# HGRN sample tokens in whole-array products: value copies by transfers, scores from the key copies, a score tile per head

## The chip, the core and the metric

The kernel runs on one core of a Trainium2 chip. The engines that matter here are TensorE (PE in the profile; its weight loads are the row PEld), VectorE (DVE), ScalarE (ACT), GpSimd (POOL) and SyncE (SP), which issues most transfers. The metric is the device time of one execution in microseconds; times are medians of several runs. TensorE is an array of 128 x 128 cells. A matrix product can use a part of it: the profile writes 128\*128 for the whole array, 32\*128 for a tile of 32 rows, 128\*32 for a tile of 32 columns.

## What is computed

One inference step of a hybrid layer: 1024 prompt tokens and 8 sample sequences of 4 tokens each (32 sample tokens), width 1024. After an RMS norm one projection feeds two groups, HGRN2 (4 heads, keys and values of 128) and a gated convolution; both are merged by the output projection. The change concerns the HGRN2 recurrence of the sample tokens. For each sequence and head, with g the running sum of log f within the 4 tokens:

```
g = cumsum(logf)
decay = exp(where(causal, g[t] - g[s], -inf))
scores[t,s] = sum_d q[t,d] k[s,d] decay[t,s,d]
o[t]  = sum_s scores[t,s] v[s]  +  (q[t] * exp(g[t])) @ s0
s_new = exp(g_last) * s0 + sum_s (k[s] * exp(g_last - g[s])) v[s]^T
```

The eight sequences are independent of one another; each begins from a state s0 that is an input.

## The kernel before

Everything lies with features on the 128 partitions and tokens along the free axis: 1024 prompt columns and 32 sample columns beside them, cut into three blocks of 352 for a projection. The input projection runs as 24 blocks of 128 output features (`order`: gates and values of the convolution gb and ga, forget f and query q per head, then za and zb), each a sum of 72 products in `fp32r` (weights and inputs are split into a high and a low part, three products each). Weights come by one transfer a block (`load_w`), are cast to the high part by ScalarE and reduced to the low part by VectorE. Four PSUM banks (`mm`) hold the projections, two (`aux`) the small products, one each `ops` and `ptps`.

Beside the projections run two lists of work written as Python generators: `hq`, the HGRN heads (`hgrn`), and `bg`, the convolution and its norm. After each third of a projection `pump` takes three steps (`HU`) of the first list, and steps of the second as long as a modelled clock of VectorE is not too far ahead of TensorE's. A step ends at a `yield`. What is emitted in this order is then placed by a planner, which simulates the engines with its own costs: earlier emitted work goes first where it is ready, and each engine keeps the planned order. Buffers of a tag are handed out in the order of emission.

A head first does the prompt in two halves of 512 tokens, stores the prompt's state, and then does the sample part:

- it loads the eight states s0 (tile `raw`, a single buffer, which later also holds blocks of the output weights);
- `ki` holds g less its last value per sequence; after an exponential and a product with k it is written four times side by side (`k4`, 128 x 4 x 32), and turned by TensorE, so that the four copies of the 32 tokens lie on the 128 partitions (`kT`);
- the head's values lie in 32 rows of `vs` (head hd in rows 32 hd to 32 hd + 31). A product with `bones` (ones where two indices are the same token) spreads them to four copies in PSUM. ScalarE casts keys and values to `fp32r`, VectorE puts the rounding rest in some of the copies (`kT`, `vr`), so that one pass of products gives the full precision;
- the scores: `base` makes a second pair of decayed operands, from g less its value at the second token (two exponentials, a difference, two products); a product in a tile of 32 columns gives 32 x 32 scores in the head's rows, and a masked copy puts the causal ones within a sequence into `ptss`, one 128 x 32 tile for all heads;
- the outputs: a product of the head's 32 rows of `vs` with the same rows of `ptss` in a tile of 32 rows, plus what the states give (sixteen small products with `qz`, copied to `isb`, and a product with `bones`);
- the state update: the values are masked per sequence (`vm`), two products with `kT` give the sums, VectorE adds them to the decayed s0, and the result is stored.

The tiles `v4`, `k4`, `kT`, `vr` and `isb` share the tag `kts`. The output projection waits for all heads and the convolution's norm.

Of the kernel before, what the change touches and what calls it, by code (L numbers as in the profile page):

```python
# [9 lines left out]
F32 = mybir.dt.float32  # L10
BF16 = mybir.dt.bfloat16
F32R = mybir.dt.float32r
U8 = mybir.dt.uint8
I32 = mybir.dt.int32
AF = mybir.ActivationFunctionType
ALU = mybir.AluOpType
AX = mybir.AxisListType

P = 128
# [3 lines left out]
NS = 4  # L23
ST = NB * NS
# [3 lines left out]
H = 4  # L28
# [28 lines left out]
NMASK = 2 + len(LEVELS)  # L57
# [39 lines left out]
def emit(nc, tc, h, fast, flag_out=None):  # L97
    HW = 5
    with ExitStack() as ctx:
# [5 lines left out]
        def sb(shape, tag, bufs=1, dt=F32):  # L105
            return pool.tile(shape, dt, tag=tag, name=tag, bufs=bufs)
# [4 lines left out]
        def bank(tag, bufs):  # L111
            return psp.tile([P, 512], F32, tag=tag, name=tag, bufs=bufs)
# [4 lines left out]
        def aux():  # L117
            return bank("aux", 2)

        S = nc.scalar  # L120
        V, T = Clock(nc.vector, _dve_ns), Clock(nc.tensor, _pe_ns)
# [18 lines left out]
        vs = sb([P, P], "vs")  # L140
# [186 lines left out]
        smask = sb([P, nmask, ST], "smask", dt=U8)  # L327
# [16 lines left out]
        pts = [sb([P, 2, P], "pt%d" % i) for i in range(2)]  # L344
# [5 lines left out]
            nc.gpsimd.memset(t, 0.0)  # L350
        bones = sb([P, P], "bones")
        nc.sync.dma_start(bones, h["bones"])
        ptss = sb([P, ST], "pts")
        nc.gpsimd.memset(ptss, 0.0)


# [105 lines left out]
        def hgrn(hd, q, k, g):  # L462
            vcols = slice(hd * P, (hd + 1) * P)
            rows = slice(hd * ST, (hd + 1) * ST)
            ptps = late["ptps"]
            st = None
            if fast:

                gc = g[:, 0:SEQ].rearrange("p (c t) -> p c t", t=P)
                r0, r1 = rng[:, hd, 0:8], rng[:, hd, 8:16]  # L470
# [7 lines left out]
            for hf in range(2):  # L478
                c0 = hf * 512
                gv = g[:, c0 : c0 + 512]  # L480
                qv = q[:, c0 : c0 + 512]
                kv = k[:, c0 : c0 + 512]

                def hw():
                    return sb([P, 512], "hw", HW)

                def rel(blk, idx, src=gv, n=512, mk=hw):
                    d = mk()
                    v = src.rearrange("p (c t) -> p c t", t=blk)
                    V.tensor_tensor(  # L490
                        d.rearrange("p (c t) -> p c t", t=blk),
                        v,
                        v[:, :, idx : idx + 1].to_broadcast([P, n // blk, blk]),
                        ALU.subtract,
                    )
                    return d

                def level(hs, src=gv, n=512, mk=hw, qq=qv, kk=kv):
                    blk = 2 * hs
                    d = rel(blk, hs - 1, src, n, mk)  # L500
                    d3 = d.rearrange("p (c t) -> p c t", t=blk)
                    q3 = qq.rearrange("p (c t) -> p c t", t=blk)
                    k3 = kk.rearrange("p (c t) -> p c t", t=blk)
                    l, r = slice(0, hs), slice(hs, blk)
                    S.activation(d3[:, :, l], d3[:, :, l], AF.Exp, scale=-1.0)
                    S.activation(d3[:, :, r], d3[:, :, r], AF.Exp)
                    V.tensor_tensor(d3[:, :, l], d3[:, :, l], k3[:, :, l], ALU.mult)
                    V.tensor_tensor(d3[:, :, r], d3[:, :, r], q3[:, :, r], ALU.mult)
                    return d

                def base(blk, idx, src=gv, n=512, mk=hw, qq=qv, kk=kv):
                    d = rel(blk, idx, src, n, mk)
                    kb = mk()
                    S.activation(kb, d, AF.Exp, scale=-1.0)
                    S.activation(d, d, AF.Exp)
                    V.tensor_tensor(kb, kb, kk, ALU.mult)
                    V.tensor_tensor(d, d, qq, ALU.mult)
                    return d, kb
# [4 lines left out]
                if fast:  # L523


                    qb, kb = base(P, P // 2 - 1)
                    yield
                    kps = aux()
                    for c in range(4):
                        T.transpose(kps[:, c * P : (c + 1) * P], kb[:, c * P : (c + 1) * P], ident)  # L530
                    kT = sb([P, 512], "ho", 2)
                    S.copy(kT, kps)
                    for c in range(4):
# [5 lines left out]
                            start=True, stop=True,  # L539
# [3 lines left out]
                            start=True, stop=True, tile_position=(0, 64),  # L543
# [19 lines left out]
                    for c in range(4):  # L563
                        T.matmul(
                            dps[:, c * P : (c + 1) * P],
                            lhsT=kT[:, c * P : (c + 1) * P],
                            rhs=vt[:, hf * 4 + c, vcols],
                            start=True,
                            stop=True,
# [14 lines left out]
                else:  # L584
# [3 lines left out]
                    ki = hw()  # L588
# [9 lines left out]
                    kps = aux()  # L598
                    for c in range(4):
                        T.transpose(kps[:, c * P : (c + 1) * P], ki[:, c * P : (c + 1) * P], ident)  # L600
                    kT = sb([P, 512], "ho", 2)
# [3 lines left out]
                    for c in range(4):  # L605
                        T.matmul(
                            dps[:, c * P : (c + 1) * P],
                            lhsT=kT[:, c * P : (c + 1) * P],
                            rhs=vt[:, hf * 4 + c, vcols],
                            start=True,  # L610
                            stop=True,
# [14 lines left out]
                    for i, hs in enumerate(LEVELS + (0,)):  # L626
                        if hs:
                            a = b = level(hs)
                        else:
                            a, b = kv, qv  # L630
                        for c in range(4):
                            T.matmul(
                                ptps[:, c * P : (c + 1) * P],
                                lhsT=a[:, c * P : (c + 1) * P],
                                rhs=b[:, c * P : (c + 1) * P],
                                start=True,
                                stop=True,
# [15 lines left out]
                for c in range(4):  # L653
                    oc = ops[:, c * P : (c + 1) * P]
                    if sts[c] is not None:
                        T.matmul(
                            oc, lhsT=sts[c], rhs=qi[:, c * P : (c + 1) * P], start=True, stop=False
# [3 lines left out]
                        lhsT=vt[:, hf * 4 + c, vcols],  # L661
                        rhs=pts[c // 2][:, c % 2, :],
                        start=(sts[c] is None),
                        stop=True,
# [11 lines left out]
            gv, qv, kv = (t[:, SEQ:TOK] for t in (g, q, k))  # L676

            def sm():
                return sb([P, ST], "sm", 8)

            s0 = sb([P, NB, P], "raw", 1)
            nc.sync.dma_start(s0, h["sh"][hd])
            eg = sb([P, NB], "egs", 2)
            S.activation(eg, gv.rearrange("p (c t) -> p c t", t=NS)[:, :, NS - 1], AF.Exp)
            ki = rel(NS, NS - 1, gv, ST, sm)
            S.activation(ki, ki, AF.Exp, scale=-1.0)
            k4 = sb([P, 4, ST], "kts", 3)
            V.tensor_tensor(
                k4,
                ki.unsqueeze(1).to_broadcast([P, 4, ST]),  # L690
# [2 lines left out]
            )  # L693
            kps = aux()
            T.transpose(kps[:, 0:P], k4.rearrange("p a t -> p (a t)"), ident)
            T.matmul(
                kps[:, P : 2 * P],
                lhsT=bones[rows, :],
                rhs=vs[rows, :],
                start=True,  # L700
                stop=True,
                tile_position=(hd * ST, 0),
            )


            kT = sb([P, P], "kts", 3, F32R)
            vr = sb([P, P], "kts", 3, F32R)
            S.copy(kT, kps[:, 0:P])
            S.copy(vr, kps[:, P : 2 * P])
            for dst, src, r0, r1 in ((kT, 0, 2, 4), (vr, P, 1, 2), (vr, P, 3, 4)):  # L710
                rr = slice(r0 * ST, r1 * ST)
                V.tensor_tensor(
                    dst[rr], kps[rr, src : src + P], dst[rr].bitcast(F32), ALU.subtract
                )
            qi = sm()
            S.activation(qi, gv, AF.Exp)
            qz = qzs[0]
# [4 lines left out]
                ALU.mult,  # L722
            )
            yield
            sps = aux()
            if fast:
                qb, kb = base(NS, 1, gv, ST, sm, qv, kv)
                pairs = [(kb, qb)]
            else:
                pairs = []  # L730
                for hs in LEVELS[-2:]:
                    a = level(hs, gv, ST, sm, qv, kv)
                    pairs.append((a, a))
                pairs.append((kv, qv))
            for i, (a, b) in enumerate(pairs):
                sp = sps[rows, i * ST : (i + 1) * ST]
                T.matmul(sp, lhsT=a, rhs=b, start=True, stop=True, tile_position=(0, hd * ST))
                mi = 0 if fast else NMASK - 3 + i
                V.copy_predicated(ptss[rows, :], smask[rows, mi, :], sp)
            ops = bank("ops", 1)  # L740
            T.matmul(
                ops[:, 0:ST],
                lhsT=vs[rows, :],
                rhs=ptss[rows, :],
                start=True,
                stop=False,
                tile_position=(hd * ST, 0),
            )
            ips = aux()
            for b in range(NB):  # L750
                j = b % 4
                T.matmul(
                    ips[j * ST : (j + 1) * ST, 0:P],
                    lhsT=qz[:, b * ST : (b + 1) * ST],
                    rhs=s0[:, b, :],
                    start=(b < 4),
                    stop=(b >= 4),
                    tile_position=(0, j * ST),
                )
            isb = sb([P, P], "kts", 3)  # L760
            S.copy(isb, ips[:, 0:P])
            T.matmul(ops[:, 0:ST], lhsT=isb, rhs=bones[:, 0:ST], start=False, stop=True)
            yield
# [486 lines left out]
def program(nc, tc, h, fallback=True):  # L1250
    with tc.tile_pool(name="flag", bufs=1) as fp:
        flag = fp.tile([1, 1], I32, name="flag")
        emit(nc, tc, h, True, flag)
        if fallback:
            slow = nc.values_load(flag[0:1, 0:1], min_val=0, max_val=1)
            with tc.If(slow > 0):
                emit(nc, tc, h, False)
# [98 lines left out]
```

## Time and profile before

| What | us |
|---|---|
| median of 3 runs | 500.35 (499.99 to 501.29) |
| the profiled execution | 500.03 |
| its span | 498.2 |
| the sample products of the four heads begin at | 184.2, 242.9, 309.2, 361.8 |
| first load of output weights issued (L1085) | 356.2 |

The mean granted clock of TensorE was 0.993. A row of the timeline gives the start, the length, the engine, the line (for most operations the line of a helper, L72), the operation, the tile written and the tiles read, the form and the number of instructions merged into the row; in brackets stands the idle time of the engine before it and what ended it. "issue" means that the engine waited for nothing that the profile shows. A product in full f32 appears as two instructions, one in `fp32r` as one. A group row gives smallest, median and largest length in ns, and the first and last start.

### The profile page before, as it was taken

The page shows a single profiled execution, that of the slowest core. Times are in us where ns is not written, and L with a number is a line of the kernel's source. Part 1 is how long each engine was busy: PE and PEld are TensorE (multiplying, and loading weights), DVE is VectorE, ACT ScalarE, POOL GpSimd, SP SyncE. Part 2 cuts the span into 40 slices and gives each one's busy share as a digit, 9 for nine tenths or more (in the row PEclk, how much of TensorE's full clock was granted, in tenths as well). Part 3 has the DMA queues.
Part 4 walks back from the last instruction along what each step waited for, and adds up shares of the span by engine and source line. Part 5 has one row for each costly group of instructions (what it writes and reads, how often), then busy time and mean ns, then how long its engine had stood idle before and what let it go on. Part 6 is the DMA issues. An engine that isn't in the chain of part 4 may idle for free.

```text
span 498.2 us, 7600 instructions
## 1 busy us (share of the span) xinstructions
PE 484.2 (97%) x3020; PEld 442.7 (89%) x3020; DVE 358.6 (72%) x682; ACT 250.6 (50%) x439; POOL 3.0 (1%) x20
## 2 busy tenths in 40 slices
PE   6999999999999999999999999999999999999992
PEld 5788899999999998999999999999999977877781
DVE  4864213999999989998999988993677747543441
ACT  5764332413646554635536554545766985422321
POOL 1000000000000000000000000000000000000000
PEclk9999999999999999999999999999999999999997
DMA  7910501231111213211123101131115396432111
GB/s 272 314 43 13 170 25 30 42 62 36 42 44 43 52 49 61 88 43 43 48 55 128 27 27 49 42 128 44 47 43 180 89 415 202 153 114 86 42 53 49
DMA packets 23003, 43.52 MB, mean 87 GB/s; under 512 B 10640, under 2 KB 11920, under 8 KB 22960
## 3 DMA queue, kind: packets, MB, share of 16 engines
q1 hardware_dynamic: 21808, 40.86, 26.3%
q10 hardware_dynamic: 1152, 2.10, 1.1%
q8 instruction: 25, 0.41, 0.3%
q14 instruction: 18, 0.15, 0.1%
HBM read 35.72 MB, written 7.24 MB: 86 GB/s over the span
## 4 chain that ended last, share of the span: by engine, by line
PE 90%; ACT 4%; DMA 3%; DVE 2%; issue 1%; SPq 0%; DVEq 0%
PE mm L72 70%; PE ops L72 8%; PE ptps L72 6%; PE aux L72 5%; DMA u<-gin 1%; ACT big L954 1%; DMA raw<-wo 1%; DMA o_hs<-raw 1%; DVE raw L72 1%; ACT L455 1%; DVE qkg L72 0%; ACT big L1100 0%; DVE big L72 0%; ACT qkg L455 0%; DVE u L72 0%
## 5 line engine op out<-in xcount | busy, mean ns | idle before, releaser
L72 PE MATMUL mm<-big,wh 128*128 128x352 f32 (+1 forms) x1280 | 323.7, 332 | 0.0
L72 PEld LDWEIGHTS mm<-big,wh 128*128 128x128 f32 x1280 | 224.1, 188 | 8.1 <-issue 1.6
L72 PE MATMUL mm<-big,wl 128*128 128x352 f32 (+1 forms) x640 | 211.4, 331 | 0.0
L72 PEld LDWEIGHTS mm<-big,wl 128*128 128x128 f32 x640 | 120.5, 188 | 3.4 <-issue 0.4
L72 DVE TENSOR_TENSOR wl<-wraw,wh 128x1024 fp32r<-128x1024 f32 x24 | 29.3, 1222 | 25.9 <-ACT wh L390 25.8
L72 DVE SCALAR_TENSOR_TENSOR big<-u,wsum,big 128x511 f32<-128x511 f32 (+14 forms) x60 | 44.5, 741 | 0.6
L72 DVE SCALAR_TENSOR_TENSOR big<-u,cols,big 128x511 f32<-128x511 f32 (+14 forms) x60 | 44.0, 735 | 0.0
L72 DVE SCALAR_TENSOR_TENSOR cq<-u,cols,cq 128x511 f32<-128x511 f32 (+13 forms) x56 | 41.2, 735 | 0.0
L72 DVE TENSOR_TENSOR qkg<-mm,big 128x512 f32<-128x512 f32 x16 | 10.9, 690 | 35.7 <-PE mm L72 35.7
L390 ACT CAST wh<-wraw 128x1024 fp32r<-128x1024 f32 x24 | 25.1, 1047 | 17.2 <-issue 7.8
L72 PE MATMUL mm<-vt,wh 128*128 128x512 f32 x64 | 25.6, 402 | 0.4 <-ACT wh L1167 0.4
L395 ACT ACT_TABLE_LOAD x20 | 25.7, 1283 | 0.3
L455 ACT ACTIVATE qkg<-mm 128x352 f32<-128x352 f32 x48 | 19.4, 465 | 11.4 <-PE mm L72 11.3
L72 PE MATMUL mm<-vt,wl 128*128 128x512 f32 x64 | 24.8, 390 | 0.0
L1204 ACT ACTIVATE big<-qkg 128x512 f32<-128x512 f32 x16 | 10.0, 628 | 29.1 <-DVE qkg L72 29.1
L455 ACT ACT_TABLE_LOAD x16 | 20.5, 1283 | 1.3 <-PE mm L72 1.0
L72 PE MATMUL ops<-big 128*128 128x512 f32 x64 | 20.8, 403 | 0.2 <-ACT big L197 0.2
L72 PE MATMUL ptps<-big 128*128 128x512 f32 x64 | 19.9, 394 | 0.0
L1167 ACT CAST wh<-big 128x512 fp32r<-128x512 f32 x16 | 9.2, 617 | 19.1 <-PE mm L72 18.6
L72 PEld LDWEIGHTS mm<-vt,wh 128*128 128x128 f32 x64 | 12.0, 188 | 5.2 <-ACT wh L1167 1.7
L72 PE MATMUL mm<-hw,wh 128*128 128x512 f32 x40 | 15.7, 392 | 0.0
L799 ACT ACTIVATE big<-aux,eps 128x512 f32<-128x512 f32 (+1 forms) x12 | 6.7, 556 | 17.9 <-PE aux L72 17.5
(239 smaller groups left out, 634.7 us busy)
## 6 DMA issues: line engine op xcount, KB each, us to landing
wraw<-win SPq DMA_DIRECT2D x24, 512.0 KB, 3.6
wraw<-wo SPq DMA_DIRECT2D x12, 512.0 KB, 3.7
big<-xp SPq DMA_DIRECT2D x2, 2048.0 KB, 10.1
big<-xp SPq DMA_DIRECT2D x4, 512.0 KB, 10.7
raw<-sh SPq DMA_DIRECT2D x4, 512.0 KB, 3.5
o_hs<-raw SPq DMA_DIRECT2D x4, 512.0 KB, 3.0
raw<-wo SPq DMA_DIRECT2D x4, 512.0 KB, 5.2
o_yp<-qkg ACTq DMA_DIRECT2D x8, 256.0 KB, 2.9
```

What stands on the lines that cost most here:

```text
L72: return f(*a, **k)
L390: S.copy(hi, wr)
L395: after(S.preload_act_table_set("natural_log_exp_and_others"), prev)
L455: return [S.activation(dst[:, nb * MB : (nb + 1) * MB], ps, func, bias=bias)]
L799: S.activation(r, ms[:, 0:n], AF.Ln, bias=eps)
L954: return S.activation(cv[:, c, cs], cv[:, c, cs], AF.Silu, bias=cols[:, C_LNB + c : C_LNB + c + 1], scale=cols[:, C_LNG + c : C_LNG + c + 1],)
L1167: S.copy(hv, m[:, :, ts])
L1204: S.activation(xr[:, hs], y[:, hs], AF.Square, accum_out=sqs[:, half : half + 1])
```

## The change

The values are no longer spread by a product: four transfers within SBUF copy the head's 32 rows of `vs` to a tile `v4`, ahead of a new `yield`. The scores take the four key copies `k4` as the stationary side, so that the product uses all 128 columns and gives the same scores in four groups of rows; only the head's own rows are copied out. The moving side is a new `qe`, the query times the exponential of `ki`. The score tile gets a place of 32 columns for each head and is zero outside the head's rows, so that the output product can run over all 128 rows of `vs`. The tag `kts` gets a fourth buffer. The fallback path (`fast` false) is kept to the same layout; it isn't executed with these inputs.

```diff
-        ptss = sb([P, ST], "pts")
+
+        ptss = sb([P, H, ST], "pts")
         nc.gpsimd.memset(ptss, 0.0)
...
             s0 = sb([P, NB, P], "raw", 1)
             nc.sync.dma_start(s0, h["sh"][hd])
+
+            v4 = sb([P, P], "kts", 4)
+            for j in range(4):
+                nc.sync.dma_start(v4[j * ST : (j + 1) * ST, :], vs[rows, :])
+            yield
             eg = sb([P, NB], "egs", 2)
             S.activation(eg, gv.rearrange("p (c t) -> p c t", t=NS)[:, :, NS - 1], AF.Exp)
             ki = rel(NS, NS - 1, gv, ST, sm)
+            if fast:
+                qe = sm()
+                S.activation(qe, ki, AF.Exp)
+                V.tensor_tensor(qe, qe, qv, ALU.mult)
             S.activation(ki, ki, AF.Exp, scale=-1.0)
...
             kps = aux()
             T.transpose(kps[:, 0:P], k4.rearrange("p a t -> p (a t)"), ident)
-            T.matmul(
-                kps[:, P : 2 * P],
-                lhsT=bones[rows, :],
-                rhs=vs[rows, :],
-                start=True,
-                stop=True,
-                tile_position=(hd * ST, 0),
-            )
...
-            S.copy(vr, kps[:, P : 2 * P])
...
+            if fast:
+
+                sps = kps[:, P : P + ST]
+                T.matmul(
+                    sps, lhsT=k4.rearrange("p a t -> p (a t)"), rhs=qe, start=True, stop=True
+                )
+                V.copy_predicated(ptss[rows, hd, :], smask[rows, 0, :], sps[rows, :])
...
+            S.copy(vr, v4)
...
-            sps = aux()
-            if fast:
-                qb, kb = base(NS, 1, gv, ST, sm, qv, kv)
-                pairs = [(kb, qb)]
...
             ops = bank("ops", 1)
             T.matmul(
                 ops[:, 0:ST],
-                lhsT=vs[rows, :],
-                rhs=ptss[rows, :],
+                lhsT=vs,
+                rhs=ptss[:, hd, :],
                 start=True,
                 stop=False,
-                tile_position=(hd * ST, 0),
             )
```

More of the change, by code (lines that the diff above doesn't have):

```diff
@@ L685, in hgrn @@
             ki = rel(NS, NS - 1, gv, ST, sm)
+            if fast:
+                qe = sm()
+                S.activation(qe, ki, AF.Exp)
+                V.tensor_tensor(qe, qe, qv, ALU.mult)
             S.activation(ki, ki, AF.Exp, scale=-1.0)
-            k4 = sb([P, 4, ST], "kts", 3)
+            k4 = sb([P, 4, ST], "kts", 4)
             V.tensor_tensor(
@@ L695, in hgrn @@
             T.transpose(kps[:, 0:P], k4.rearrange("p a t -> p (a t)"), ident)
-            T.matmul(
-                kps[:, P : 2 * P],
-                lhsT=bones[rows, :],
-                rhs=vs[rows, :],
-                start=True,
-                stop=True,
-                tile_position=(hd * ST, 0),
-            )
-            kT = sb([P, P], "kts", 3, F32R)
-            vr = sb([P, P], "kts", 3, F32R)
+            if fast:
[4 more added lines that the diff above has]
+                V.copy_predicated(ptss[rows, hd, :], smask[rows, 0, :], sps[rows, :])
+            vr = sb([P, P], "kts", 4, F32R)
+            S.copy(vr, v4)
+            kT = sb([P, P], "kts", 4, F32R)
             S.copy(kT, kps[:, 0:P])
-            S.copy(vr, kps[:, P : 2 * P])
-            for dst, src, r0, r1 in ((kT, 0, 2, 4), (vr, P, 1, 2), (vr, P, 3, 4)):
+            for dst, src, r0, r1 in ((kT, kps, 2, 4), (vr, v4, 1, 2), (vr, v4, 3, 4)):
                 rr = slice(r0 * ST, r1 * ST)
-                V.tensor_tensor(
-                    dst[rr], kps[rr, src : src + P], dst[rr].bitcast(F32), ALU.subtract
-                )
+                V.tensor_tensor(dst[rr], src[rr, 0:P], dst[rr].bitcast(F32), ALU.subtract)
             qi = sm()
@@ L724, in hgrn @@
             yield
-            sps = aux()
-            if fast:
-                qb, kb = base(NS, 1, gv, ST, sm, qv, kv)
-                pairs = [(kb, qb)]
-            else:
+            if not fast:
+                sps = aux()
                 pairs = []
@@ L734, in hgrn @@
                 pairs.append((kv, qv))
[L735 to L739, printed above, removed]
+                for i, (a, b) in enumerate(pairs):
+                    sp = sps[rows, i * ST : (i + 1) * ST]
+                    T.matmul(sp, lhsT=a, rhs=b, start=True, stop=True, tile_position=(0, hd * ST))
+                    V.copy_predicated(ptss[rows, hd, :], smask[rows, NMASK - 3 + i, :], sp)
             ops = bank("ops", 1)
@@ L759, in hgrn @@
                 )
-            isb = sb([P, P], "kts", 3)
+            isb = sb([P, P], "kts", 4)
             S.copy(isb, ips[:, 0:P])
```

## The prediction

> **What bounds the kernel now.** I read the page's busy line first, then the shares of the chain that ended last, then the table of stages, and last the timeline of TensorE around one head's sample part.
>
> ```profile
> PE 484.2 (97%) x3020; PEld 442.7 (89%) x3020; DVE 358.6 (72%) x682; ACT 250.6 (50%) x439; POOL 3.0 (1%) x20
> PE 90%; ACT 4%; DMA 3%; DVE 2%; issue 1%; SPq 0%; DVEq 0%
> 180.00:200.00 20.00, 20.00 (x144) 18.15 (x143) 18.75 (x41) 9.20 (x17) 0.12 (x1) 1.00 0.31 68
> ```
>
> TensorE is busy for 97% of the span and makes 90% of the last chain. The third line is the stage in which head 0's sample tokens are worked on (columns: window; its length; busy us and instructions of PE, PEld, DVE, ACT, POOL; granted clock; DMA share; GB/s): PE has no idle time at the full clock. VectorE, at 18.75 of 20 us, is close behind. So what the change is worth there is what it takes out of TensorE's row of products, as long as nothing else takes the lead.
>
> "Busy" hides something. A projection's wide products (352 columns) start every 0.16 us, a 512-column product takes 0.23 us to the next start, yet around small tiled products the row stretches. I price each small product by that stretch: from the last wide start ahead of it to the second wide start behind it, less what the same wide products take undisturbed.
>
> ```profile
> 184.24 0.27 PE L72 MATMUL aux<-ident,kts 128*128 128x128 f32 x1
> 184.44 0.48 PE L72 MATMUL aux<-vs,bones 32*128 32x128 f32 x2
> 184.85 0.43 PE L72 MATMUL mm<-big,wh 128*128 128x352 f32 x1
> 185.12 0.32 PE L72 MATMUL mm<-big,wl 128*128 128x352 f32 x1
> ...
> 189.38 0.32 PE L72 MATMUL mm<-big,wh 128*128 128x352 f32 x1
> 189.63 0.25 PE L72 MATMUL aux<-sm 128*32 128x32 f32 x2
> 189.81 0.43 PE L72 MATMUL mm<-big,wh 128*128 128x352 f32 x1
> 190.07 0.33 PE L72 MATMUL mm<-big,wl 128*128 128x352 f32 x1
> 190.24 0.48 PE L72 MATMUL mm<-big,wh 128*128 128x352 f32 x2
> 190.65 0.64 PE L72 MATMUL aux<-raw,qz 128*32 128x128 f32 x16
> ...
> 191.49 0.48 PE L72 MATMUL mm<-big,wh 128*128 128x352 f32 x2
> ...
> 193.24 0.32 PE L72 MATMUL mm<-big,wl 128*128 128x352 f32 x1
> 193.49 0.40 PE L72 MATMUL ops<-pts,vs 32*128 32x32 f32 x2
> 193.83 0.50 PE L72 MATMUL aux<-hw,kts 128*128 128x512 f32 x1
> 194.16 0.48 PE L72 MATMUL mm<-big,wh 128*128 128x352 f32 x2
> ...
> 194.96 0.32 PE L72 MATMUL mm<-big,wl 128*128 128x352 f32 x1
> 195.12 0.32 PE L72 MATMUL mm<-big,wh 128*128 128x352 f32 x1
> 195.29 0.30 PE L72 MATMUL ops<-bones,kts 128*128 128x32 f32 x2
> 195.42 0.47 PE L72 MATMUL aux<-hw,kts 128*128 128x512 f32 x1
> ```
>
> This is TensorE's timeline for head 0 (start, length, then the product; 32*128 and 128*32 are the rows and columns of the array in use; an f32 product shows as two). 194.96 to 195.12 is the wide step, 0.16. The reader should see that every block with less than 128*128 has a gap of 0.25 us ahead of it instead of 0.16 and a late second wide product behind it, while the one small pair on the whole array (bones,kts) has neither.
>
> ```profile
> 329.01 0.60 PE L72 MATMUL aux<-ident,hw 128*128 128x128 f32 x4
> 329.37 0.40 PE L72 MATMUL mm<-big,wl 128*128 128x352 f32 x1
> 329.61 0.48 PE L72 MATMUL mm<-big,wh 128*128 128x352 f32 x2
> ...
> 361.78 0.27 PE L72 MATMUL aux<-ident,kts 128*128 128x128 f32 x1
> ...
> 366.90 0.49 PE L72 MATMUL mm<-big,wh 128*128 128x352 f32 x2
> 367.31 0.22 PE L72 MATMUL aux<-sm 128*32 128x32 f32 x1
> ...
> 368.20 0.48 PE L72 MATMUL mm<-big,wh 128*128 128x352 f32 x2
> ...
> 371.38 0.39 PE L72 MATMUL aux<-hw,kts 128*128 128x512 f32 x1
> 371.61 0.32 PE L72 MATMUL mm<-big,wl 128*128 128x352 f32 x1
> ```
>
> **The change part by part, on TensorE.**
> Spreading product (bones by vs), removed. From the transpose at 184.24 to the second wide start at 185.12 are 0.88 us. A transpose followed by wide products alone: four transposes from 329.01 last 0.60, one lasts 0.27, so the last starts at 329.34, and 329.61 is the second wide start: 0.27. The product costs 0.61, in four heads 2.44.
> Scores, from a column tile to the whole array. 189.38 to 190.07 is 0.69; two wide steps are 0.32: it costs 0.37. Head 3 is different: its pair stands in one block with the sixteen state products (raw,qz) and shares their gaps. From the second wide start ahead (0.16 behind 366.90) to 368.20 are 1.14; head 0's state products alone take from 190.40 to 191.49, 1.09. So head 3 loses only 0.05. Charging heads 1 and 2 as head 0: 3 x 0.37 + 0.05 = 1.16.
> Outputs (pts by vs), from a 32-row tile to the whole array. 193.24 to 194.16 is 0.92; one wide step and one 512-column step (371.38 to 371.61, 0.23) are 0.39: it costs 0.53, in four heads 2.12.
> Removed together: 2.44 + 1.16 + 2.12 = 5.72 us.
> Added: eight pairs of 32 columns on the whole array. The nearest row is bones,kts, the same shape: 195.12 to 195.42 is 0.30, less one step of 0.16 is 0.14. Eight make 1.12. The floor is head 3's 0.05 a pair (0.4), the ceiling the tiled pair's 0.53 (4.2); I take 0.14, since shape and array are the same.
> Net on TensorE: 5.72 - 1.12 = **4.6 us less**; with the ends of the added pairs 1.5 to 5.3.
>
> The page TensorEngine Tiling (Array Packing) of the Trainium skill speaks against the change in its section Overview: with a contraction or a moving side of at most 64 the whole array is underused, and tiles of 32 could be up to four times as fast. Its section Tiling Modes speaks for it: changing the mode drains the engine. The rows above agree with the second: no two of these tiles run side by side, so each pays its two changes of mode and gains nothing. By the first alone, read as whole-array pairs no cheaper than the tiled ones, the sum would be 1.5 us instead of 4.6; that case is a rival below.
>
> **The other engines.** VectorE loses two 32-column products a head (one difference and one product; three go, one comes), ScalarE one 32-column exponential.
>
> ```profile
> L72 DVE TENSOR_TENSOR sm<-sm,qkg x8: 182/187/195, 140.9 to 280.9; 128x32 f32<-128x32 f32 x8
> 182.31 0.33 SPq L387 DMA_DIRECT2D wraw<-win  x1
> 190.81 1.03 ACT L390 CAST wh<-wraw 128x1024 fp32r<-128x1024 f32 x1
> wraw<-win SPq DMA_DIRECT2D x24, 512.0 KB, 3.6
> raw<-smask SPq DMA_DIRECT2D x1, 16.0 KB, 1.8
> ```
>
> 2 x 4 x 0.187 is 1.5 us of VectorE. I count it at nothing: VectorE is beside TensorE, not ahead of it. That it drops by 1.5 while TensorE drops by 4.6 narrows its margin. The first row shows where these operations run: from 140.9, over 40 us ahead of head 0's products at 184, so the scores' new operand will be waiting when the transpose comes. Copying the values to rounded form from SBUF rather than PSUM leaves the count of casts and differences unchanged; I take no gain or loss. The larger zero fill of the score tile is on POOL (1% busy) at the start: nothing.
>
> Transfers: four of 16 KB a head, sixteen in all, on SyncE's queue. The trace has none within SBUF. Lower end: nothing, hidden; the nearest row is the mask's 16 KB, 1.8 us to landing. On the queue each takes about the 0.33 us of the weight load's issue row, 1.3 us a head. Queued behind them are the weight loads. One issued at 182.31 lands some 3.6 us later, at 185.9, and ScalarE casts it at 190.81: 4.9 us of cover. So 1.3 us is hidden; upper end, were the cover gone, 4 x 1.3 = 5.2 us. The transfers wait for a free `kts` buffer. With five tiles a head in four buffers the next head's copy takes one that the transpose or the cast has left long before, and the values have been there since the first stage; I take nothing. ScalarE's cast of the copied values waits for them; queued behind it are the casts of weights and the reading of projections, for which TensorE waits. The margin is the same tens of us between load and use.
>
> **What moves.** The new stop (yield) pushes the key transpose, the scores and the new query product one step of the head's list later, so they are issued at the same pump as the outputs, a third of a projection later. The state update (fourteenth step before, fifteenth after) stays in the same pump, as three steps are taken at each.
>
> ```profile
> 373.73 1.90 DVE raw L72 x7
> 375.65 3.27 DMA o_hs<-raw
> 378.94 4.00 DMA raw<-wo
> ...
> 402.61 0.50 PE L72 MATMUL mm<-vt,wh 128*128 128x512 f32 x1 [0.41 <-ACT wh L1167]
> ```
>
> Why this matters stands in the chain of head 3: its state update frees the only `raw` buffer, after the store, for a row block of the output weights, whose cast holds ScalarE; and the first output products wait 0.41 us for ScalarE at 402.61. That path has no slack. If head 3's update stays at its place in TensorE's row, the whole path moves up with it and the 4.6 us reach the end; if it comes later in the row by d, the end moves by d less.
>
> **Sum.** The profiled execution took 500.03 us, its span 498.2, with 1.83 around it; minus 4.6 it is 495.4. The median of the three runs is 500.35, 0.3 above it, so the forecast is **495.8 us**.
>
> **The rivals.**
> Part of it is given back at the join (A). Transpose, cast, difference and state product, 9.6 us apart for head 3 now (361.8 to 371.4), fall into one pump; TensorE's row has few places to hide a VectorE that is 94% busy. For: VectorE's load. Against: ScalarE and VectorE take part in that path for under 1 us in all, and one PSUM tile fewer is asked for per head. With 1 to 3.5 us lost: 496.8 to 499.3.
> The whole array is the dearer form (C): eight pairs at 0.53. The net is 1.5 us: 498.9. Against: the bones,kts rows. This is what the underuse rule of the Trainium skill's page on tiling would make of it.
> Slower (B). Head 3's state update moves with its transpose, which goes from 361.8 to the pump of 367.3: 5.5 us later in the row. Then store, load of `wo` and ScalarE's casts are 5.5 later against a row 4.6 shorter: 0.9 us slower, 501.3, and more if the other `wo` loads queue behind the store. It decides from a delay of 4.6 us on. For: no slack at 402.61. Against: the update's pump does not change, by the count of steps.
> The change doesn't do what it says: the gaps belong to small f32 products, not to tiles. That is C with the same price, and the same row speaks against it.
>
> **How the numbers follow.** Forecast (495 to 496.6) 0.57, A 0.20, C 0.05, B 0.12, and 0.06 for an order of work that the planner changes elsewhere, to either side. 0.3% is 1.5 us, about what a measurement of this kernel can tell from no change. Faster by more than that (under 498.85): the forecast, most of A, half of C and of the rest, 0.76. Within: the end of A, half of C, much of B, 0.15. Slower (over 501.85): the far part of B and the rest, 0.09. The range runs from 494.8 (pairs at the floor, 5.3 us) to 499.3 (the end of A), which leaves out B and little else.
>
> **What would show it.** Right: vs,bones gone from TensorE's groups; the scores and outputs as 128*128 pairs with a stretch near 0.14; tiled products left only as raw,qz in the sample part; PE still without idle time from 110 to 375; the first out-products still waiting under 1 us near 398. Wrong: new waits of TensorE for `kts` or `pts` writers, weight casts waiting for DMA, a wait of several us near 398 behind `raw<-wo`, or stretches of 0.5 around the whole-array pairs.

## The result and the profile after

| | us |
|---|---|
| before, median of 4 runs | 500.52 (499.99 to 501.29) |
| changed, median of 4 runs | 496.4 (495.68 to 497.04) |
| ratio | 0.9913, interval 0.9894 to 0.9933 |
| profiled execution of the changed kernel | 497.04, span 495.3 |

The change takes 4.1 us off; forecast were 4.7 (495.8 against 500.5), with a range of 494.8 to 499.3. From the page of the changed kernel come the busy line and the shares of the last chain, then the stage of head 0's sample part in the table of stages:

```profile
PE 480.6 (97%) x3012; PEld 442.2 (89%) x3012; DVE 357.1 (72%) x674; ACT 250.1 (50%) x435; POOL 4.1 (1%) x20
PE 91%; DMA 3%; ACT 2%; DVE 2%; issue 0%; SPq 0%; DVEq 0%
```

```profile
190.00:210.00 20.00, 20.00 (x149) 18.97 (x147) 19.78 (x45) 11.32 (x20) 0.12 (x1) 1.00 0.29 71
```

TensorE is as full as before and still carries the end. VectorE has come closer (19.78 of 20 us), and TensorE still doesn't wait for it. These are the largest waits of TensorE in the whole span (who waited for whom, us in total, times, longest):

```profile
PE mm L72 <- DVE raw L72: 1.8, 1, 1.8
PE mm L72 <- DVE avg L132: 1.6, 1, 1.6
PE ops L72 <- DVE qkg L72: 1.0, 1, 1.0
PE mm L72 <- ACT qkg L456: 0.4, 1, 0.4
```

The first three lie in the first 13 us, at 8.24, 1.63 and 12.00; from 14 us on the one wait of 0.1 us or more is that of 0.4, at 384.06. Now TensorE's timeline where the scores and outputs of heads 0 and 2 stand:

```profile
192.57 0.39 PE L72 MATMUL aux<-ho,avg 128*128 128x512 f32 x1
192.80 0.27 PE L72 MATMUL aux<-ident,kts 128*128 128x128 f32 x1
192.91 0.31 PE L72 MATMUL aux<-sm,kts 128*128 128x32 f32 x2
193.05 0.57 PE L72 MATMUL mm<-big,wh 128*128 128x352 f32 x2
...
201.60 0.32 PE L72 MATMUL mm<-big,wh 128*128 128x352 f32 x1
201.76 0.30 PE L72 MATMUL ops<-pts,vs 128*128 128x32 f32 x2
201.90 0.41 PE L72 MATMUL mm<-big,wh 128*128 128x352 f32 x1
202.15 0.32 PE L72 MATMUL mm<-big,wl 128*128 128x352 f32 x1
...
317.57 0.64 PE L72 MATMUL aux<-raw,qz 128*32 128x128 f32 x16
318.14 0.41 PE L72 MATMUL ops<-pts,vs 128*128 128x32 f32 x2
318.39 0.48 PE L72 MATMUL aux<-hw,kts 128*128 128x512 f32 x1
```

All scores and outputs run on the whole array, the transpose goes straight into the scores, and of the sample part nothing has a gap of 0.25 ahead of it any more but the state products (raw,qz). But the pair isn't free of a mark behind it: from the last wide start ahead (201.60) to the second behind (202.15) are 0.55; less two steps, 0.32, it costs 0.23 and not 0.14. The first wide product follows the pair after 0.14, and the second comes 0.25 behind the first.

To see where the time went, I set the same products of two traces side by side: the first and the last (1728th) wide product of the projections, and a product late in the output projection (the 337th of its 512-column products). The shift of the first is the start, what is added up to the last is the **row**, what is added from there on is the **join**, the step from the projections to the output projection:

| kernel | start | row | join | function tables loaded by ScalarE |
|---|---|---|---|---|
| changed, against before | +1.36 | -4.33 | 0.00 | 43, as before |

The start's 1.36 comes and goes from one profiled execution to the next (-0.4 to +1.7 over all that follow). Ahead of it lie only the larger zero fill and the first head's value copies, and a later kernel with both and the same order of products (nine stops more) starts at +0.13. So the two profiled executions differ by 3.0 us, and the row's 4.33 is the change.

### The profile page after: what moved, and what is told of

Same layout as the page of the kernel before. It is cut to its first block, busy times and chain, and to the rows that moved or that the text cites. A ratio compares the mean times of both kernels' runs of the same rounds, so it can differ in the third digit from the quotient of the medians.

```text
span 495.3 us, 7605 instructions
## 1 busy us (share of the span) xinstructions
PE 480.6 (97%) x3012; PEld 442.2 (89%) x3012; DVE 357.1 (72%) x674; ACT 250.1 (50%) x435; POOL 4.1 (1%) x20
## 4 chain that ended last, share of the span: by engine, by line
PE 91%; DMA 3%; ACT 2%; DVE 2%; issue 0%; SPq 0%; DVEq 0%
PE mm L72 71%; PE ops L72 8%; PE ptps L72 7%; PE aux L72 5%; DMA o_hs<-raw 1%; DMA u<-gin 1%; DMA raw<-wo 1%; DVE raw L72 1%; ACT L456 1%; DVE qkg L72 0%; ACT big L1102 0%; DVE u L72 0%; ACT L396 0%; ACT L943 0%; DVE big L72 0%
## 5 line engine op out<-in xcount | busy, mean ns | idle before, releaser
L882 ACT ACTIVATE u<-mm,cols 128x352 f32<-128x352 f32 (+2 forms) x16 | 6.5, 484 | 17.8 <-PE mm L72 17.8
```

What stands on the lines that cost most here:

```text
L882: out.append(S.activation(dst, src, func, bias=bias))
```

## The experiments

Each measured time is a median, with the ratio to the kernel before on the same chip and its interval. A table near the end of this section has start, row and join for all.

**The parts alone.** First the copies of the values:

```diff
+            v4 = sb([P, P], "kts", 4)
+            for j in range(4):
+                nc.sync.dma_start(v4[j * ST : (j + 1) * ST, :], vs[rows, :])
+            yield
...
-            T.matmul(kps[:, P : 2 * P], lhsT=bones[rows, :], rhs=vs[rows, :], ...)
...
+            S.copy(vr, v4)
```

> Of the change only the copies of the values: four transfers a head and the new stop in place of the spreading product; scores and outputs stay in their tiles. Theory (each tiled block costs its stretch of TensorE's row): 4 x 0.61 = 2.4 us less than before, about 498.1. Rival (the gain comes from the order of work that the planner finds, which moves with any edit): anything between no gain and the whole 4 us, with no relation to the 0.61.

Measured 510.37, 1.0185 (1.0172 to 1.0198): 9.5 us slower. The row is 2.72 shorter, where the theory has 2.4. All the loss lies at the join, 13.0 us. This is ScalarE's timeline there, and the wait of TensorE that ends it:

```profile
385.68 1.28 ACT L934 ACT_TABLE_LOAD   x1
386.98 0.50 ACT L934 ACTIVATE u<-u 128x352 f32<-128x352 f32 x1
387.49 1.28 ACT L791 ACT_TABLE_LOAD   x1
388.79 0.29 ACT L791 ACTIVATE big<-aux,eps 128x32 f32<-128x32 f32 x1
388.98 1.04 ACT L1092 CAST vt<-raw 128x1024 fp32r<-128x1024 f32 x1
390.04 1.28 ACT L455 ACT_TABLE_LOAD   x1
391.33 0.47 ACT L455 ACTIVATE qkg<-mm 128x352 f32<-128x352 f32 x1
391.81 1.28 ACT L792 ACT_TABLE_LOAD   x1
393.11 0.23 ACT L792 ACTIVATE big<-big 128x32 f32<-128x32 f32 x1
...
394.62 1.28 ACT L946 ACT_TABLE_LOAD   x1
```

```profile
400.68 0.80 PE L72 MATMUL mm<-vt,wh 128*128 128x512 f32 x1 [7.67 <-ACT wh L1159]
```

L791 and L792 are the logarithm and exponential of the last head's sample norm, 32 columns wide and half a microsecond of work; L934 is an exponential of the convolution's norm. The planner put them between the silus of the projections (L455) and of the convolution (L946), and in these rows every change of function comes with a table load of 1.28 us. TensorE, early in its row, waits 7.67 us for the cast of the first mixed outputs (L1159), which stands behind all of them.

Then the scores alone, from `k4` and `qe` into a free part of `kps`, with the spreading product and the tiled outputs left:

```diff
+                sps = kps[:, 2 * P : 2 * P + ST]
+                T.matmul(sps, lhsT=k4.rearrange("p a t -> p (a t)"), rhs=qe, start=True, stop=True)
+                V.copy_predicated(ptss[rows, :], smask[rows, 0, :], sps[rows, :])
```

> Of the change only the scores from the key copies on the whole array; the spreading product and the tiled outputs stay. By the prices of the prediction (1.16 removed, 4 x 0.14 added) 0.6 us less, 499.9. By the stretch that the changed kernel shows for such a pair, 0.23 to the second wide start behind it, 4 x 0.23 = 0.92 are added: 0.2 less, 500.3, not to be told from before. If the whole array were the dearer form (0.53 a pair): 1 us more.

Measured 506.15, 1.0118 (1.0102 to 1.0133). The row is 1.4 longer, though each pair stands on the array: the planner's order is another (13 blocks of prompt scores instead of 11 for 8 halves, the last head's state products cut in two), and TensorE waits twice for 0.9 us together. At the join 4.7 more, with 45 table loads and a wait of 3.1 us. So neither of these two prices was tested cleanly by the time; the blocks of the traces, added up below, do it.

Then the outputs alone:

```diff
-        ptss = sb([P, ST], "pts")
+        ptss = sb([P, H, ST], "pts")
...
-                lhsT=vs[rows, :], rhs=ptss[rows, :], ..., tile_position=(hd * ST, 0),
+                lhsT=vs, rhs=ptss[:, hd, :], ...
```

> Of the change only the score tile per head and the output product on the whole array. Theory with 0.23 for the new pair: 2.12 less 0.92, 1.2 us less than before, 499.3; with the prediction's 0.14 it is 1.6 less. Rival (order of work): no gain, since nothing else moves here.

Measured 499.46, 0.9972 (0.996 to 0.9984): 1.4 us less. Here the planner kept the order, so the traces can be laid over each other: the row is shorter by about 0.29 at each head's output product and by nothing between, 1.14 in all. That is 0.53 less 0.23, four times; with 0.14 it would have been 1.56.

**The stop.** The whole change without its `yield`:

```diff
                 nc.sync.dma_start(v4[j * ST : (j + 1) * ST, :], vs[rows, :])
-            yield
```

> The whole change without its new stop, so that transpose, scores and state update stand at the steps that they had before. Theory: the products are the same, so the time is that of the changed kernel within 0.5 us, about 496.4. Rival (order of work; the stop hides the transfers or moves the state update): over 1 us away from it, with ScalarE waiting for the value copies or the load of output weights later.

Measured 496.91, 0.9913 (0.9897 to 0.9928): the changed kernel's time. TensorE's order is the same from end to end; wide product by wide product the row lies a constant 0.26 later until the join, which is the start. The stop moves nothing.

**The price by itself.** 46 products that nobody reads, added to the changed kernel among the projections, in tiles and on the whole array:

```diff
                 if nb < 2 and ndrain:
+                    dps_ = aux()
+                    T.matmul(dps_[:, 0:ST], lhsT=vs[0:ST, :], rhs=bones[0:ST, 0:ST], start=True, stop=True, tile_position=(0, 0))
                     pump()
```

> The changed kernel with 46 added products whose results nobody reads, one after each of the first two thirds of 23 projections: 32 columns in a tile of 32 rows. Theory: each stretches TensorE's row by the tiled pair's 0.53, 24 us in all. Rival (small f32 products cost what they cost, tile or not): the same time as the next kernel. The planner may shift other work by a few us either way; the stretch per product is read from the trace.

The second has `lhsT=vs, rhs=bones[:, 0:ST]` and no position.

> The changed kernel with 46 added products at the same places, on the whole array (128 rows, 128 columns, 32 columns moving). Theory: 0.23 each, 11 us in all, some 14 us less than the tiled ones. By the prediction's price of 0.14 it is 6 us. Rival: the same as the tiled ones.

Measured 519.03, 1.0363 (1.033 to 1.0396), and 511.64, 1.0219 (1.0178 to 1.026): 22.6 and 15.2 us above the changed kernel. The difference of the medians, 7.4, is half of what was expected. In the profiled executions it is 10.0 (519.09 and 509.10): 11.7 in the row, less 2.1 at the join, where both lost time again (45 table loads). The four executions of the second spread from 509.1 to 513.46 us, so its median says less than the traces. In the row the tiled ones cost 21.6 and the others 9.9, on average 0.47 and 0.21 each, as some stand beside other small products. One of each alone in TensorE's timeline:

```profile
118.54 0.32 PE L72 MATMUL mm<-big,wh 128*128 128x352 f32 x1
118.80 0.40 PE L72 MATMUL aux<-bones,vs 32*128 32x32 f32 x2
119.13 0.43 PE L72 MATMUL mm<-big,wh 128*128 128x352 f32 x1
119.40 0.32 PE L72 MATMUL mm<-big,wl 128*128 128x352 f32 x1
```

```profile
116.64 0.32 PE L72 MATMUL mm<-big,wh 128*128 128x352 f32 x1
116.80 0.30 PE L72 MATMUL aux<-bones,vs 128*128 128x32 f32 x2
116.94 0.41 PE L72 MATMUL mm<-big,wh 128*128 128x352 f32 x1
117.19 0.32 PE L72 MATMUL mm<-big,wl 128*128 128x352 f32 x1
```

0.86 and 0.55 from the first row to the last, less 0.32: 0.54 and 0.23. The gap ahead and the late follower go with the tile, not with the smallness; the whole array keeps only the late follower.

**The join.** Nine stops more ahead of the last head's sample norm in the changed kernel:

```diff
+            if hd == 3:
+                for _ in range(9):
+                    yield
             yield from head_norm(hd, SEQ, ST, ops)
```

> The changed kernel, products and copies unchanged; only the norm of the last head's sample outputs is emitted nine steps (three pumps) later. Theory of the join: ScalarE's logarithm and exponential then fall among the silu evacuations, each change of function loads a table (1.28 us), and TensorE waits for the first output products near 395: two or three more table loads and 2 to 10 us more. Rival (the join follows TensorE's row): no change, 496.4.

Measured 496.0, 0.9893 (0.9864 to 0.9921). The expected loss didn't come, but neither did the late norm: 43 table loads, and TensorE's order is that of the changed kernel throughout. Like the other stop, these moved nothing, so this says nothing about the join. What does move the planner is priority. The copies alone once more, with the sample norms ahead of the evacuations:

```diff
-            yield from head_norm(hd, SEQ, ST, ops)
+            with tc.high_priority(HP):
+                for _ in head_norm(hd, SEQ, ST, ops):
+                    pass
+            yield
```

> The kernel with the value copies alone, and the norm of the sample outputs put ahead of the projections' evacuations in the planner's order. If what the copies alone lose at the join comes from the late norm among the silus: 43 table loads again instead of 46, TensorE waits under 2 us there, and the time is that of the shorter row, about 498. If it comes from the late state update and the load of output weights behind it: still over 505.

Measured 497.91, 0.9934 (0.991 to 0.9959): 12.5 us less than the copies alone, and 41 table loads. ScalarE's timeline at the same place:

```profile
379.37 0.29 ACT L794 ACTIVATE big<-aux,eps 128x32 f32<-128x32 f32 x1 [0.94 <-PE aux L72]
379.69 0.23 ACT L795 ACTIVATE big<-big 128x32 f32<-128x32 f32 x1
379.94 1.28 ACT L455 ACT_TABLE_LOAD   x1
381.23 1.18 ACT L455 ACTIVATE qkg<-mm 128x352 f32<-128x352 f32 x3
382.28 4.70 ACT L949 ACTIVATE big<-big,cols 128x352 f32<-128x352 f32 x8
386.87 0.62 ACT L1162 CAST wh<-big 128x512 fp32r<-128x512 f32 x1
387.38 1.06 ACT L1095 CAST vt<-raw 128x1024 fp32r<-128x1024 f32 x1
```

The norm stands ahead of the silus; its logarithm and exponential follow each other without a load, and three silus of the projections and eight of the convolution run behind one. The last row matters for the prediction: it is the cast of the output weights that wait for the `raw` buffer. Here is the same cast before and in the changed kernel:

```profile
382.96 1.05 ACT L1100 CAST vt<-raw 128x1024 fp32r<-128x1024 f32 x1 [2.75 <-DMA raw<-wo]
```

```profile
381.19 1.05 ACT L1102 CAST vt<-raw 128x1024 fp32r<-128x1024 f32 x1 [2.49 <-DMA raw<-wo]
```

With the copies and the norm ahead it comes 4.4 us later than before, though the row is 3.3 shorter, and the join costs 0.2. Its load, behind the state update and the store, was issued 2.2 us later (381.13 against 378.94). So a late state update alone doesn't hurt. The five loads saved are 6.4 of the 12.8 us that the join gained; the rest I didn't take apart.

For the scores alone I tried the convolution's norm instead, whose logarithm and exponential stood between the silus in that run (`LHP = 4000` in place of 2000).

> The kernel with the scores alone on the whole array, and the convolution's norm put ahead of the projections' evacuations in the planner's order (in the run with the scores alone its logarithm and exponential stood between silu evacuations, with 45 table loads instead of 43, and TensorE waited 3.1 us for the mixed output's cast). If the loss of the scores alone sits in that order: under 502.5, with the pairs on the array unchanged. If the whole-array scores themselves cost it, or the planner finds no better order: still about 506.

Measured 506.74, 1.0105 (1.0081 to 1.0129): the edit moved nothing, TensorE's order is that of the scores alone throughout, with the same 45 loads and wait of 3.1 us. So it says nothing on the cause, and why the scores alone lose at the join stays open. And the whole change with the sample norm ahead, the edit of the copies' second run:

> The whole change with the norm of the sample outputs ahead of the projections' evacuations. Its join already costs under 0.5 us, so there is little to gain: 495.5 to 496.8, the changed kernel's time. If the planner's order of the join was an unlucky one there too: 1 us or more less.

Measured 500.66, 0.9977 (0.9959 to 0.9996). The same row, 4.42 shorter, and now it is the changed kernel that loses at the join, 3.5 us, with 45 loads. No order of the norm is good for all.

**The same idea further.** The prompt's scores on the whole array too:

```diff
-                        T.matmul(
-                            ptps[0:64, cs], lhsT=kb[:, c * P : c1], rhs=qb[:, cs], ...
-                        T.matmul(
-                            ptps[64:P, c1:ce], lhsT=kb[:, c1:ce], rhs=qb[:, c1:ce], ...
+                        T.matmul(
+                            ptps[:, cs], lhsT=kb[:, cs], rhs=qb[:, cs], start=True, stop=True,
...
-                    S.activation(d, d, AF.Exp)
+                    S.activation(d, d, AF.Exp, bias=lnc)
...
-            S.activation(r, ms[:, 0:n], AF.Ln, bias=eps)
+            S.activation(r, ms[:, 0:n], AF.Ln, bias=eps, scale=1.0 / (c * c))
```

> The changed kernel with the prompt's scores on the whole array as well: four products of 128 columns a half instead of eight in column tiles of 64. The query side carries a factor 2^-24, taken out again in the norm, so that the unused corner of the scores stays finite. Theory: a tiled block now stretches the row by 0.25 + 1.02 + 0.27 less 0.32, 1.22 us; eight instructions of 0.11 and the end of a pair make about 0.95; eight halves save 2.2 us, about 494.2. Rival (order at the join): up to 13 us more, as the value copies alone showed.

> The same with the sample norm ahead of the evacuations: if the join is what can spoil it, this one is near 494 even where the one before is not.

Measured 494.79, 0.9877 (0.9859 to 0.9895), and with the norm ahead 497.18, 0.9917 (0.9899 to 0.9935). The first is clearly faster than the kernel before. Its median is 1.6 us below the changed kernel's, measured on another occasion, and 1.2 below that with nine stops more; the intervals of the ratios overlap, so that it beats the changed kernel is likely and not shown. A half's scores in TensorE's timeline, in the changed kernel and then in the first of these two:

```profile
147.54 0.32 PE L72 MATMUL mm<-big,wh 128*128 128x352 f32 x1
147.80 1.09 PE L72 MATMUL ptps<-hw 128*64 128x128 f32 x16
148.81 0.43 PE L72 MATMUL mm<-big,wh 128*128 128x352 f32 x1
149.08 0.32 PE L72 MATMUL mm<-big,wl 128*128 128x352 f32 x1
```

```profile
146.26 0.32 PE L73 MATMUL mm<-big,wh 128*128 128x352 f32 x1
146.42 1.05 PE L73 MATMUL ptps<-hw 128*128 128x128 f32 x8
147.23 0.41 PE L73 MATMUL mm<-big,wh 128*128 128x352 f32 x1
147.48 0.33 PE L73 MATMUL mm<-big,wl 128*128 128x352 f32 x1
```

1.22 less 0.32 is 0.90 in place of 1.54 less 0.32, 1.22. One half is still cut by other products, but on the whole array the cut costs nothing more (1.34 for both together, of which the other products take 0.45 alone). The row is 3.95 shorter than the changed kernel's, not 2.2; the join takes 2.9 of it back (45 loads), so the time came near the expected one by two misses that nearly cancel. The second lost more there (3.7) and started later.

All runs against the kernel before, in us from their profiled executions:

| kernel | start | row | join | table loads |
|---|---|---|---|---|
| changed | +1.36 | -4.33 | 0.00 | 43 |
| copies alone | +0.06 | -2.72 | +13.02 | 46 |
| scores alone | +0.12 | +1.39 | +4.71 | 45 |
| outputs alone | +0.68 | -1.14 | -0.43 | 43 |
| without the stop | +1.62 | -4.31 | +0.02 | 43 |
| 46 tiled products added | -0.08 | +17.24 | +1.93 | 45 |
| 46 on the whole array added | -0.43 | +5.52 | +4.00 | 45 |
| nine stops more | +0.13 | -4.24 | +0.07 | 43 |
| copies alone, norm ahead | -0.03 | -3.31 | +0.21 | 41 |
| scores alone, other norm ahead | +1.72 | +1.41 | +4.75 | 45 |
| changed, norm ahead | +0.15 | -4.42 | +3.53 | 45 |
| prompt's scores too | +0.08 | -8.28 | +2.93 | 45 |
| the same, norm ahead | +1.60 | -8.13 | +3.66 | 45 |

The join costs nothing with 41 or 43 loads and 2 to 13 us with 45 or 46. One pair of runs (the copies) shows that the place of the norm in the order is the cause; for the others it is only this agreement.

The prices of the parts can be added up from the traces themselves. Each block of products between wide ones is priced by the prediction's rule, less two steps of 0.16; a prompt block or a product of the convolution's norm that stands in the same block is taken out at its own price. All blocks with sample products (transpose, spreading, scores, states, outputs, and the 512-column products in the same blocks) take together:

| kernel | sample blocks, us |
|---|---|
| before | 12.94 |
| changed | 8.98 |
| copies alone | 10.85 |
| scores alone | 13.03 |
| outputs alone | 11.75 |

In the copies alone the transpose stands without the spreading product:

```profile
190.87 0.27 PE L72 MATMUL aux<-ident,kts 128*128 128x128 f32 x1
...
191.15 0.33 PE L72 MATMUL mm<-big,wl 128*128 128x352 f32 x1
```

0.28 from the transpose to the second wide start, against 0.88 before: 0.60 a head for the spreading product. In all the copies save 2.09, since the last head's scores now stand by themselves and cost 0.38 there instead of 0.05. In the scores alone a pair on the whole array adds 0.22 to its block (1.17 against 0.95), but the last head's state products, cut in two, cost 0.33 more, and nothing is saved. The outputs save 1.19.

## Why the prediction came out right, step by step

**Direction and size.** Right: 4.1 us measured, 4.6 worked out. The lower end of the range is a slip: with the floor of 0.4 for the added pairs, 5.3 us less, it is 495.1 and not 494.8.

**What was removed.** Right: the spreading product at 0.61 a head came back as 0.60 in the copies alone, the tiled output pair at 0.53 as 0.54 in the added products. The tiled scores take 0.38 wherever they stand alone, but had no added product of their own.

**What was added.** The term that was mis-sized: a pair on the whole array at 0.14. The row chosen (bones,kts) was right, but I read it to the first start behind it, not to the second, against my own rule, because a 512-column product followed. With 0.23 eight pairs are 1.84, not 1.12, and the sum is 5.72 - 1.84 = 3.9. The sample blocks give 12.94 - 8.98 = 3.96. The row gave 4.33, and the rest is no price of the change: in the changed kernel the prompt's blocks take 0.4 less (10 blocks of scores instead of 11), a small tiled product (aux<-ident,lmin, 0.51) has passed behind the last wide product, and the wait at 384.06 costs 0.65, together some 0.3 less. That is counted from the trace and not shown by a run of its own; with the norm ahead the row is as short with 13 blocks.

**The transfers.** Mis-sized and without effect. In the changed kernel's groups and waits of the tile:

```profile
L687 SPq DMA_DIRECT2D kts<-vs x16: 507/590/665, 52.6 to 315.8; - x16
...
  DMA kts<-vs: 5.3, 1
...
DMA to landing us min/median/max: 2.2/3.8/5.3
```

An issue takes 0.59 us, not 0.33, and landing 3.8, not 1.8. The margin of tens of us held only for the first head, whose copies are issued at 52.6 and cast at 140.4. The others stand in the queue among weight loads and are issued from 195.63, 254.48 and 313.94, 7 to 11 us ahead of their casts (204.09, 261.65, 325.12). ScalarE waited once, 5.3 us, for the third head's, of which the last was issued at 257.08, behind a weight load. TensorE didn't wait at all.

**What moves.** Wrong. I had the stop push the transpose to a later pump and kept the state update in place; the runs without the stop and with nine more show the planner's order unchanged. Things did move: head 0's transpose from 184.24 to 192.80, head 3's from 361.78 to 359.25, and the store behind head 3's state update is issued 4.1 us earlier (371.59 against 375.65), 1.1 more than the end of the row. But they do so without the stop too, so another part of the change does it; which, no run shows.

**The join.** The place was right, the mechanism wrong. "That path has no slack" doesn't hold: in the changed kernel the cast behind `raw` moved up by 1.8 us where the row's end moved up by 3.0, and the join lost nothing; with the copies and the norm ahead it even came later than before and 0.2 was lost. In the copies alone, what cost time there was the place of the norm in ScalarE's order. The Trainium skill (ScalarE: Activation LUTs, section Table sets: the hidden batching unit) says to batch activations by table set; the two runs of the copies agree, with 46 loads and 510.37 us against 41 and 497.91. Rival A (part given back at the join) did not occur in the changed kernel, whose join is 0.00, nor did B. Two of the three parts alone came out slower than before, as B has it, but by another way than B's, with 13.0 and 4.7 us lost at the join. So the forecast's 0.57 leaned on luck that its profile couldn't show: that the planner would find an order with 43 loads.

**The page on tiling.** The rule that changing the mode drains the engine (the Trainium skill, TensorEngine Tiling (Array Packing), section Tiling Modes) agrees with the added products: the same pair costs 0.54 in a tile and 0.23 on the whole array. The underuse that its Overview speaks of didn't show, as the changed tiles did not run side by side (but for the last head's scores, which stood among its state products). The sixteen state products kept their tiles: before, sixteen of 128 columns last 0.64 us together, four transposes of 128 columns on the whole array 0.60.

## What to carry to other kernels

A lone small product in a tile of the array costs more than the same product padded with zeros to the whole array, here 0.3 us for 32 rows and 0.15 for 32 columns; count the blocks of tiled products, not their size, and price each from the last undisturbed start ahead to the second one behind. In a kernel whose order a planner makes, split the time at the engine's own landmarks before judging an edit: here parts that shortened the bounding row came out up to 9.5 us slower, where in the one case that a second run settles another engine's order had changed at one place. Watch there how often ScalarE loads a table.

## What the hardware showed beyond that

A long wait of TensorE can cost more than its length. In the copies alone the wait of 7.67 us goes with a granted clock of 0.87 over the stage from 380 to 420, where before, the changed kernel and the outputs alone have 1.00 (the scores alone, with a wait of 3.1 us, 0.96):

```profile
380.00:420.00 40.00, 30.45 (x145) 25.94 (x145) 21.21 (x33) 30.58 (x43) 0.00 (x0) 0.87 0.54 197
```

The trace shows the place: from 396.6 us, within the wait, to 406.8 the granted clock is 0.50, and 512-column products start 0.43 us apart until it is full again, where 0.23 is usual. In the runs with waits of 2.6 to 3.1 us for the mixed outputs' cast (the scores alone, the same with the other norm ahead, the changed kernel with the norm ahead) the clock is at 0.50 for 3.4 us; the 46 products on the whole array, with a wait of 1.98 us there, kept 1.00.
